# Four edits to a two-layer decoder trunk: padded arrays, joint splits of activations, one load on another queue, and two matmuls exchanged

## The chip, the cores and the metric

The kernel runs on one core of a Trainium2 chip. The metric is the device time of one execution in microseconds (us); before the change the median of three executions is 2053.09 us. The profile below is of one execution whose instructions span 2049.4 us. On the core, TensorE (PE) multiplies matrices and loads their stationary operands (PEld), VectorE (DVE) and ScalarE (ACT) do the elementwise work, GpSimd (POOL) does almost nothing, and SyncE (SP) issues the transfers.

## The reference, cut to what matters

```python
# D_MODEL 2048, SEQ 256, DEPTH 2, D_FF 8192, all float32
for layer in range(DEPTH):
    if layer < N_A:
        mix = short_conv_mixer(h, conv_w_in[layer], conv_w[layer], conv_w_out[layer])
    else:
        if layer == N_A:
            k_nope, k_pe, v = shared_latent_kv(h, kv_w_dkv, kv_norm_g, kv_w_ukv, cos, sin)
        mix = mla_mixer(h, ...)                       # 16 heads, causal softmax
    h = layer_norm(ALPHA * h + mix, ln_g[layer, 0], ln_b[layer, 0])
    h = layer_norm(ALPHA * h + sq_relu_mlp(h, mlp_w1[layer], mlp_w2[layer]), ...)

def sq_relu_mlp(x, w1, w2):
    return jnp.square(jax.nn.relu(x @ w1)) @ w2
```

The first layer mixes with a gated short convolution (projections of 2048 by 6144 and 2048 by 2048), the second with latent attention. Each has an MLP with 2048 by 8192 and 8192 by 2048 weights. Nearly all the work is in the products, and they run in float32.

## The kernel before, in words

**Products in two parts.** Every operand of a product is split into a rounded high part (type fp32r, made by a copy on ACT, line 111) and the low remainder (a subtraction on DVE, line 112; `split`). A product is then three terms, high by high, high by low and low by high. With the activations held as 512 columns, 256 high and 256 low, one K tile of 128 rows costs two matmuls: `high` (line 190, the weight's high part against all 512 columns) and `low` (line 194, the weight's low part against the first 256). `mm_run` runs 16 such pairs for one unit, 128 output rows; `whole` (lines 300 to 304) adds the two halves of the bank when it is done.

**Stages.** The input projection of the convolution has 48 units, the first three of them run side by side, on the input held in the arrays tagged a1 and a2 (8 K tiles each); its output projection has 16 units on z, in the array tagged b. An MLP goes over the 8192 hidden columns in 8 passes (`q` 0 to 7) of 8 units. The activations x are in the array tagged b, the hidden values of a pass in c. Pass 0 uses another form of product (`mm_wide`). The passes 1 to 7 call `products`, W1 for short below; after the W1 units of a pass come its W2 products, with the hidden values as stationary operand and 512 columns of weights moving (`dot`, lines 247 to 249). In the passes named in `FAST`, 1 to 6 of the first MLP and 1 to 7 of the second, half the W2 columns go through a product of the Strassen and Winograd kind, `down_fast`: seven products instead of eight for each pair of hidden tiles, over four pairs (`ps_f`, 84 matmuls). The other columns take the plain way (`down`, `ps_d`, 96 matmuls).

**Who prepares what.** `prepare` loads a weight (512 KB, line 132, on the SP queue) and splits it. For a pair of `down_fast` it loads two and forms combinations of them first: `raw_t`, two subtractions in `raw`, four splits, the last of which is written as `t` and is what the pair's first product reads. `hidden` (line 558) takes a unit out of its bank, applies relu and square, splits the result (`put_split`, lines 308 and 309) and, for every second unit of a FAST pass, forms four sums of the pair's quarters (lines 570 to 573, tile `sf`) and splits these, 512 columns, into `forms` (tag a2).

**Order.** The program is written stage by stage, but a planner orders each engine's instructions, and those of the SP queue, by simulated readiness. On the chip each engine and each queue takes its instructions strictly in the planned order.

**Where the arrays lie.** One pool holds, one after another, the residual (16,384 bytes for each partition), a1, a2, b, c, some arrays of 1,024 or 2,048 bytes, then the raw weights and the split weights (4,096 bytes each). A tag is as large as its largest user: 16,512 bytes for a1 and a2, 33,024 for b, 16,384 for c. So, modulo 512 bytes and counted from the residual, a1 begins at 0, a2 at 128, b at 256, c and the split weights at 0. Small constants stand ahead of the pool (`vec` 736 bytes, `col` 16), small statistics behind it, and behind these the tiles `sf` and `t4` of the FAST passes, where `t4` begins at 384.

**The end.** In the last pass, `to_out` first loads the gain and bias of the last norm, broadcast to all partitions, into the array tagged b (`gbt`, four transfers of 512 KB, line 869, on the POOL queue). It must wait for the last W1 matmul, which reads x from b. Then come `down_fast`, the rest of W2, and the norm.

Of the kernel before, what the change touches and what calls it, by code (L numbers as in the profile page):

```python
# [15 lines left out]
P = 128  # L16
# [24 lines left out]

C_G, C_B, C_CW, C_QG, C_KG, C_END = 0, 64, 128, 176, 180, 184
# [3 lines left out]
def trunk(ctx: ExitStack, tc: tile.TileContext, xT, vecs, w_in, w_out, w_kv, w_q, w_uk, w_uv,  # L46
# [10 lines left out]


# [171 lines left out]
    def products(n, x, group=0, cuts=()):  # L230
# [20 lines left out]
    def held(x, t):  # L251

        return [x[:, o + t * P:o + (t + 1) * P] for o in (0, T)]
# [33 lines left out]
    def down_fast(x, forms):  # L287
# [3 lines left out]
        for j in range(n):  # L291
            b, = take(1)
            a = {"11": held(x[2 * j], 0), "12": held(x[2 * j + 1], 0), "22": held(x[2 * j + 1], 1)}
            for i in range(4):
                a[f"S{i + 1}"] = [forms[:, j, o, i * P:(i + 1) * P] for o in range(2)]
# [16 lines left out]
    vec = const.tile([P, C_END], F32, name="vec")  # L312
# [5 lines left out]
    col = const.tile([P, 4], F32, name="col")  # L318
# [28 lines left out]
    class Norm:  # L347
# [35 lines left out]
        def widen(self, *tags):  # L383
# [4 lines left out]
            for i, tag in enumerate(tags):  # L388
                x = act.tile([P, n, 2 * W], F32R, tag=tag, name=f"xd{self.idx}_{i}")
# [85 lines left out]
    xhl = [t[:, k, :] for t in [act.tile([P, NC // 2, 2 * T], F32R, tag=a, name=f"xhl0_{a}") for a in ("a1", "a2")]  # L475
           for k in range(NC // 2)]

    first = act.tile([P, 2 * GROUP, 1024], F32, tag="b", name="first")
# [14 lines left out]
    zt = act.tile([P, NC, 2 * T], F32R, tag="b", name="z")  # L493
    z = [zt[:, k, :] for k in range(NC)]
    cbuf = act.tile([P, 2, 5, T + 2], F32, tag="c", name="cbuf")
# [27 lines left out]
    def mlp(idx, ln, begin, blocks, fast):  # L523
# [3 lines left out]
        xt = act.tile([P, NC, 2 * T], F32R, tag="b", name=f"xhl{idx}")  # L527
# [20 lines left out]
        for q in range(NQ):  # L548
            ht = act.tile([P, QC, 2 * T], F32R, tag="c", name=f"h{idx}_{q}")
            h = [ht[:, k, :] for k in range(QC)]  # L550
            forms = None
            if q in FAST[idx // 2]:
                forms = act.tile([P, QC // 2, 2, 4 * P], F32R, tag="a2", name=f"forms{idx}_{q}")
            if q == NQ - 1:
                begin(block)
            pair = []

            def hidden(m, ps, evac, *func):
                f = tmp.tile([P, T], F32, tag="fh", name="fh", bufs=3)
# [4 lines left out]
                put_split(h[m], f)  # L564
                pair.append(f)
                if forms is not None and m % 2:
                    (a11, a21), (a12, a22) = ((v[:, :P], v[:, P:]) for v in pair[-2:])
                    sf = fast.tile([P, 4, P], F32, tag="sf", name="sf")
                    s1, s2, s3, s4 = (sf[:, i, :] for i in range(4))
                    nc.vector.tensor_tensor(s1, a21, a22, ALU.add)  # L570
                    nc.vector.tensor_tensor(s3, a21, a11, ALU.subtract)
                    nc.vector.tensor_tensor(s2, s1, a11, ALU.subtract)
                    nc.vector.tensor_tensor(s4, a12, s2, ALU.subtract)
                    split(forms[:, m // 2, 0, :], forms[:, m // 2, 1, :], sf.rearrange("p i c -> p (i c)"))

            if q == 0:
# [15 lines left out]
                acc = act.tile([P, 2, D], F32, tag="a1", name=f"acc{idx}")  # L592
            else:
                for m, ps in enumerate(products(QC, xhl)):
# [56 lines left out]
    with tc.tile_pool(name="att", bufs=1) as ap:  # L651
        lat = act.tile([P, 2 * NK, 2 * T], F32R, tag="c", name="lat")
# [81 lines left out]
        ot = act.tile([P, H, 2 * T], F32R, tag="b", name="oT")  # L734
        oT = [ot[:, k, :] for k in range(H)]
        kq, vp = (act.tile([P, NC * W], F32, tag=a, name=f"kqv{a}") for a in ("a1", "a2"))
# [248 lines left out]
```

## Time and profile before

| | us |
|---|---|
| median of three executions | 2053.09 (2053.00 to 2053.85) |
| span of the profiled execution | 2049.4 |
| PE busy | 2030.6 |
| DVE busy | 1662.8 |
| ACT busy | 1194.1 |

The profiled execution's own time is known by its span alone. The median of the timed executions stands 3.7 us above that span; this is taken as what lies around the instructions, and any sum on the span has to have it added. A matmul's row in a timeline gives its start, its modelled duration and its kind. Matmuls overlap in the array, so the pace is read from start to start, and not from durations.

### The profile page before, as it was taken

Reading aid. Unit: us, or ns where it says so; the run is one execution under the profiler, and the core shown is the slowest. Engines: PE = TensorE matmul, PEld = TensorE weight load, DVE = VectorE, ACT = ScalarE, POOL = GpSimd, SP = SyncE. Lnnn points to the kernel's source line nnn. Section 1 sums busy time; section 2 is a strip of 40 time slices with the busy share of each in tenths; the row PEclk is TensorE's granted clock in tenths of the full one; section 3 lists DMA queues with packets and bytes.
Section 4 is the critical chain, followed back from the end, with each engine's and each line's share of the span. In section 5 each row is a group of like instructions: output and inputs, shape, how many; then the busy total and the mean of one; then the engine's idle time right before and its main releaser. Section 6 shows DMA issues by size and latency. Waiting matters only on the chain.

```text
span 2049.4 us, 30194 instructions
## 1 busy us (share of the span) xinstructions
PE 2030.6 (99%) x11208; PEld 1760.4 (86%) x11208; DVE 1662.8 (81%) x2602; ACT 1194.1 (58%) x1860; POOL 4.5 (0%) x25
## 2 busy tenths in 40 slices
PE   9999999999999999999999999999999999999997
PEld 8888888988888888888889998898888888888885
DVE  7667677678898988989788878776879888898988
ACT  6444445676566565655656665566656656566562
POOL 0000000000000000000000000000000000000000
PEclk9999999999999999999999999999999999999998
DMA  8666666564746557465755544656475664756653
GB/s 308 202 188 187 186 185 194 159 211 136 249 142 223 193 167 250 143 226 173 234 169 164 166 124 142 197 174 196 138 236 161 196 218 156 243 153 217 212 165 137
DMA packets 108003, 385.32 MB, mean 188 GB/s; under 512 B 11984, under 2 KB 13392, under 8 KB 107856
## 3 DMA queue, kind: packets, MB, share of 16 engines
q1 hardware_dynamic: 107136, 381.04, 58.7%
q0 software_dynamic: 576, 2.10, 0.3%
q8 instruction: 88, 1.44, 0.3%
q14 instruction: 59, 0.48, 0.1%
q10 hardware_dynamic: 144, 0.26, 0.0%
HBM read 381.25 MB, written 2.10 MB: 187 GB/s over the span
## 4 chain that ended last, share of the span: by engine, by line
PE 97%; DVE 1%; DMA 1%; issue 0%; ACT 0%; SPq 0%; DVEq 0%
PE ps_u L190 34%; PE ps_u L194 17%; PE ps_d L248 7%; PE ps_d L247 7%; PE ps_d L249 7%; PE ps_f L249 4%; PE ps_f L248 4%; PE ps_f L247 4%; PE ps_w L224 1%; PE ps_w L222 1%; PE ps_w L223 1%; PE ps_g L222 1%; PE ps_g L224 1%; PE ps_g L223 1%; PE ps_wo L190 1%; PE S L788 1%
## 5 line engine op out<-in xcount | busy, mean ns | idle before, releaser
L112 DVE TENSOR_TENSOR lo<-raw,hi 128x1024 fp32r<-128x1024 f32 x712 | 861.7, 1221 | 299.0 <-ACT hi L111 294.3
L111 ACT CAST hi<-raw 128x1024 fp32r<-128x1024 f32 x712 | 742.2, 1049 | 526.6 <-PE ps_u L190 289.5
L190 PE MATMUL ps_u<-xhl,hi 128*128 128x512 f32 x1792 | 632.2, 398 | 0.0
L194 PE MATMUL ps_u<-xhl,lo 128*128 128x256 f32 x1792 | 503.0, 281 | 0.0
L190 PEld LDWEIGHTS ps_u<-xhl,hi 128*128 128x128 f32 x1792 | 336.5, 188 | 82.3
L194 PEld LDWEIGHTS ps_u<-xhl,lo 128*128 128x128 f32 x1792 | 338.5, 189 | 0.5
L190 PE MATMUL ps_u<-xhl_a,hi 128*128 128x512 f32 x720 | 253.4, 396 | 0.0
L248 PE MATMUL ps_d<-lo,h 128*128 128x512 f32 x608 | 236.9, 390 | 0.0
L249 PE MATMUL ps_d<-hi,h 128*128 128x512 f32 x608 | 236.8, 390 | 0.0
L247 PE MATMUL ps_d<-hi,h 128*128 128x512 f32 x608 | 236.6, 389 | 0.0
L194 PE MATMUL ps_u<-xhl_a,lo 128*128 128x256 f32 x720 | 202.9, 282 | 0.0
L190 PEld LDWEIGHTS ps_u<-xhl_a,hi 128*128 128x128 f32 x720 | 135.2, 188 | 31.9
L194 PEld LDWEIGHTS ps_u<-xhl_a,lo 128*128 128x128 f32 x720 | 135.8, 189 | 0.0
L248 PEld LDWEIGHTS ps_d<-lo,h 128*128 128x128 f32 x608 | 114.1, 188 | 24.2 <-DVE lo L112 0.4
L247 PEld LDWEIGHTS ps_d<-hi,h 128*128 128x128 f32 x608 | 114.2, 188 | 24.0
L249 PEld LDWEIGHTS ps_d<-hi,h 128*128 128x128 f32 x608 | 114.1, 188 | 23.9
L111 ACT CAST hi_t<-raw_t 128x1024 fp32r<-128x1024 f32 x52 | 54.8, 1054 | 77.8 <-PE ps_u L190 41.8
L190 PE MATMUL ps_u<-z,hi 128*128 128x512 f32 x256 | 89.0, 392 | 0.0
L562 ACT ACTIVATE fh<-fh 128x256 f32<-128x256 f32 x112 | 46.4, 414 | 72.0 <-DVE fh L304 72.0
L222 PE MATMUL ps_w<-xd,hi 128*128 128x258 f32 x256 | 72.5, 284 | 0.0
L224 PE MATMUL ps_w<-xd,hi 128*128 128x258 f32 x256 | 72.5, 285 | 0.0
L223 PE MATMUL ps_w<-xd,lo 128*128 128x258 f32 x256 | 72.3, 282 | 0.0
(235 smaller groups left out, 3254.8 us busy)
## 6 DMA issues: line engine op xcount, KB each, us to landing
raw<-in_w_dram SPq DMA_DIRECT2D x408, 512.0 KB, 4.4
raw<-in_w2f_dram SPq DMA_DIRECT2D x104, 512.0 KB, 3.6
raw<-in_w_in_dram SPq DMA_DIRECT2D x90, 512.0 KB, 4.2
raw<-in_w_out_dram SPq DMA_DIRECT2D x32, 512.0 KB, 3.6
raw<-in_w_o_dram SPq DMA_DIRECT2D x32, 512.0 KB, 3.9
raw<-in_w_kv_dram SPq DMA_DIRECT2D x10, 512.0 KB, 4.3
raw<-in_w_q_dram SPq DMA_DIRECT2D x8, 512.0 KB, 4.5
raw<-in_w_uk_dram SPq DMA_DIRECT2D x8, 512.0 KB, 4.4
```

The source lines that it names most:

```text
L111: nc.scalar.copy(hi, src)
L112: nc.vector.tensor_tensor(lo, src, hi.bitcast(F32), ALU.subtract)
L190: nc.tensor.matmul(ps, w[blk // 8][0][:, blk % 8, :], x, start=first, stop=False)
L194: nc.tensor.matmul(ps[:, :T], w[blk // 8][1][:, blk % 8, :], x[:, :T], start=False, stop=last)
L222: nc.tensor.matmul(ps[:, :W], hi, x[k][:, :W], start=k == 0, stop=False)
L223: nc.tensor.matmul(ps[:, :W], lo, x[k][:, :W], start=False, stop=False)
L224: nc.tensor.matmul(ps[:, :W], hi, x[k][:, W:], start=False, stop=k == NC - 1)
L247: nc.tensor.matmul(ps, x[0], w[0], start=first, stop=False)
L248: nc.tensor.matmul(ps, x[0], w[1], start=False, stop=False)
L249: nc.tensor.matmul(ps, x[1], w[0], start=False, stop=last)
L562: nc.scalar.activation(f, f, AF.Relu)
L788: nc.tensor.matmul(S[:, at:at + n], qp[:, tok], kp[:, :n], start=False, stop=True)
```

## The change

**Arrays.** `array` gives each tag a fixed room that is a multiple of 512 bytes (16,896, 16,896, 33,280 and 16,384), and `vec`, `col` and `stats` are enlarged. The scratch for software transfers shrinks from 16,384 bytes to 2,048. All arrays of the main pool, the split weights and the FAST tiles then begin at the same offset modulo 512.

**Common splits.** In the passes 1 to 7 the two hidden tiles of a pair and the four sums are neighbours in one tile of 1,024 columns, and are split together: one copy on ACT and one subtraction on DVE instead of three each. High parts go to the array c and low parts to a2. In the one pass without sums (the first MLP's last) the pair's 512 columns are split together. The pair's tile has one buffer.

**One load on another queue.** The four `gbt` transfers go from the POOL queue to the SP queue.

**The exchange.** `products` passes `turn=2` for the first unit of the MLP passes 1 to 7: its third K tile has `low` ahead of `high`. That concerns 14 of the units.

```diff
+    ROOM = {"a1": 16896, "a2": 16896, "b": 33280, "c": 16384}
+    def array(tag, dtype, name, *dims):
+        n = int(np.prod(dims))
+        t = act.tile([P, ROOM[tag] // 4], dtype, tag=tag, name=name)[:, :n]
...
-    def mm_run(wps, x, k0, k1, nk, tiles_first=False):
+    def mm_run(wps, x, k0, k1, nk, tiles_first=False, turn=None):
...
         for k, (w, ps) in order:
+            if k == turn:
+                low(ps, w, k, x[k], False)
+                high(ps, w, k, x[k], False)
+                continue
             high(ps, w, k, x[k], k == 0)
             low(ps, w, k, x[k], k == nk - 1)
...
-            mm_run([(w, ps)], x, 0, NC, NC)
+            mm_run([(w, ps)], x, 0, NC, NC, turn=turn if i == 0 else None)
...
-    vec = const.tile([P, C_END], F32, name="vec")
+    vec = const.tile([P, 2 * P], F32, name="vec")[:, :C_END]
...
-    col = const.tile([P, 4], F32, name="col")
+    col = const.tile([P, COL], F32, name="col")
...
+            forms = [array(a, F32R, f"h{idx}_{q}_{a}", QC // 2, 8 * P) for a in ("c", "a2")] if q else None
...
-                put_split(h[m], f)
-                pair.append(f)
-                if forms is not None and m % 2:
-                    (a11, a21), (a12, a22) = ((v[:, :P], v[:, P:]) for v in pair[-2:])
-                    sf = fast.tile([P, 4, P], F32, tag="sf", name="sf")
...
-                    split(forms[:, m // 2, 0, :], forms[:, m // 2, 1, :], sf.rearrange("p i c -> p (i c)"))
+                if forms is None:
+                    put_split(h[m], f)
+                elif m % 2:
+                    hi, lo = (v[:, m // 2, :] for v in forms)
+                    src, cols = state["pair"], 4 * P
+                    if q in FAST[idx // 2]:
+                        cols = 8 * P
...
+                    split(hi[:, :cols], lo[:, :cols], src[:, :cols])
...
-                for m, ps in enumerate(products(QC, xhl)):
+                for m, ps in enumerate(products(QC, xhl, turn=2)):
...
-            nc.gpsimd.dma_start(gbt[:, n, :], gb[n].partition_broadcast(P))
-        stats = small.tile([P, 2, NB, 6], F32, tag="stats", name="stats", bufs=1)
+            nc.sync.dma_start(gbt[:, n, :], gb[n].partition_broadcast(P))
+        stats = small.tile([P, 2, NB, 10], F32, tag="stats", name="stats", bufs=1)[:, :, :, :6]
...
-    nc = _bacc.Bacc("TRN2", target_bir_lowering=False, num_devices=1)
+    nc = _bacc.Bacc("TRN2", target_bir_lowering=False, num_devices=1, dynamic_dma_scratch_size=2048)
```

More of the change, by code (lines that the diff above doesn't have):

```diff
@@ L228, in group_of, with products @@
         return [(take(), psum("ps_g")) for _ in range(n)]
-    def products(n, x, group=0, cuts=()):
+    def products(n, x, group=0, cuts=(), turn=None):
         ws = group_of(group)
@@ L294, in down_fast @@
             for i in range(4):
-                a[f"S{i + 1}"] = [forms[:, j, o, i * P:(i + 1) * P] for o in range(2)]
+                a[f"S{i + 1}"] = [v[:, j, (4 + i) * P:(5 + i) * P] for v in forms]
             for p, l, r in FACTORS:
@@ L523, in mlp @@
     def mlp(idx, ln, begin, blocks, fast):
-        xt = act.tile([P, NC, 2 * T], F32R, tag="b", name=f"xhl{idx}")
+        xt = array("b", F32R, f"xhl{idx}", NC, 2 * T)
         xhl = [xt[:, k, :] for k in range(NC)]
```

54 lines of the change are left out of this document (31 added, 23 removed).

## The prediction

> **What bounds the kernel now.** I read the page first: the shares of the engines and the chain that ended last.
>
> ```profile
> span 2049.4 us, 30194 instructions
> PE 2030.6 (99%) x11208; PEld 1760.4 (86%) x11208; DVE 1662.8 (81%) x2602; ACT 1194.1 (58%) x1860; POOL 4.5 (0%) x25
> ...
> PE 97%; DVE 1%; DMA 1%; issue 0%; ACT 0%; SPq 0%; DVEq 0%
> ```
>
> The chain is matmuls for 97% of the span, so an edit pays where it alters the pace of the matmuls or one of the few places where they wait. Hence the second view, PE's timeline, read from start to start. It is shown where a W2 stretch ends and a pass of W1 begins.
>
> ```profile
> 458.46 0.39 PE L249 MATMUL ps_d<-hi,h 128*128 128x512 f32 x1
> 458.69 0.39 PE L190 MATMUL ps_u<-xhl,hi 128*128 128x512 f32 x1
> ...
> 459.03 0.40 PE L190 MATMUL ps_u<-xhl,hi 128*128 128x512 f32 x1
> ...
> 459.38 0.40 PE L190 MATMUL ps_u<-xhl,hi 128*128 128x512 f32 x1
> ...
> 459.74 0.40 PE L190 MATMUL ps_u<-xhl,hi 128*128 128x512 f32 x1
> ...
> 460.09 0.40 PE L190 MATMUL ps_u<-xhl,hi 128*128 128x512 f32 x1
> ```
>
> Only the high matmul of each K tile is shown; a low one lies between. From the second K tile (459.03) on, three K tiles take 0.35, 0.36 and 0.35 us, 1.06 together and 0.353 each. The same instructions run faster elsewhere. Here are the first matmul of a K tile and the same place 16 K tiles, one unit, later, in a usual pass and in the first MLP's last:
>
> ```profile
> 740.83 0.40 PE L190 MATMUL ps_u<-xhl,hi 128*128 128x512 f32 x1
> ...
> 746.48 0.40 PE L190 MATMUL ps_u<-xhl,hi 128*128 128x512 f32 x1
> ...
> 1000.40 0.39 PE L190 MATMUL ps_u<-xhl,hi 128*128 128x512 f32 x1
> ...
> 1005.95 0.39 PE L190 MATMUL ps_u<-xhl,hi 128*128 128x512 f32 x1
> ```
>
> That is 5.65 us a unit against 5.55, with nothing waiting in either. So the pace of high and low in turn has a slow pattern and an even one, and which one runs depends on how a stretch was entered. The 12 passes that follow W2 without a gap (1 to 6 of both MLPs) are in the slow one; the last pass of each MLP starts after other work and is in the even one.
>
> **The exchange of two matmuls** neither adds nor removes work. It can only change the pattern. If it takes, each of the 12 passes gains 8 units x 0.10 = 0.8 us, 9.6 us in all. The nearest rows are two places where two low matmuls already stand together (a row with x2):
>
> ```profile
> 13.75 0.40 PE L194 MATMUL ps_g<-xhl_a,lo 128*128 128x256 f32 x2
> ...
> 15.04 0.40 PE L190 MATMUL ps_g<-xhl_a,hi 128*128 128x512 f32 x1
> ...
> 16.10 0.40 PE L190 MATMUL ps_g<-xhl_a,hi 128*128 128x512 f32 x1
> ...
> 284.38 0.40 PE L194 MATMUL ps_u<-z,lo 128*128 128x256 f32 x2
> ...
> 284.61 0.40 PE L190 MATMUL ps_u<-z,hi 128*128 128x512 f32 x1
> ...
> 284.96 0.39 PE L190 MATMUL ps_u<-z,hi 128*128 128x512 f32 x1
> ```
>
> After the first, three K tiles again take 1.06 us (15.04 to 16.10): nothing won. After the second a K tile takes 0.35 (284.61 to 284.96) and the duration drops to the even pattern's 0.39. One for and one against; in the change two high matmuls follow the two low ones, which neither row has. I take the gain in full, since the even pattern is the one that holds wherever a stretch on the arrays b was entered with a break, and keep nothing as the other end. The two passes that are even already may fall into the slow pattern: 0 to +1.6 us, taken as 0.
>
> **Padding.** `ps_f` is where operands with different offsets meet: `forms` lies 128 bytes off the weights modulo 512, `t4` 384, while in `ps_d` both operands are at 0.
>
> ```profile
> 763.44 0.39 PE L247 MATMUL ps_f<-t,h 128*128 128x512 f32 x1
> ...
> 782.93 0.40 PE L247 MATMUL ps_d<-hi,h 128*128 128x512 f32 x1
> ...
> 1499.64 0.39 PE L249 MATMUL ps_d<-hi,h 128*128 128x512 f32 x1
> ...
> 1505.99 0.39 PE L247 MATMUL ps_d<-hi,h 128*128 128x512 f32 x1
> ```
>
> The 84 matmuls of `ps_f` take 19.49 us, 0.232 each. The 28 of `ps_d` from 1499.64 to 1505.99 take 0.2268 each, with the same 512 moving columns. If equal offsets bring `ps_f` to that pace it takes 19.05, and some 0.05 for finding it: 0.39 less in each of 12 passes, 4.7 us (the thirteenth is below). The lower bound is nothing.
>
> The convolution's input has its second half in a2, also 128 off.
>
> ```profile
> 75.44 0.40 PE L190 MATMUL ps_u<-xhl_a,hi 128*128 128x512 f32 x1
> ...
> 81.07 0.40 PE L190 MATMUL ps_u<-xhl_a,hi 128*128 128x512 f32 x1
> ```
>
> A unit takes 5.63 there. With equal offsets it should have one of the two patterns: the slow 5.65 (45 units x 0.02 = +1.0 us) or the even 5.55 (-3.6). I take the slow one, which its aligned first half already shows, and keep both ends.
>
> A rule of the Trainium skill speaks against this part: "SBUF — State Buffer", section "Who interferes with whom", gives PE two independent read ports and says that PE never waits on anyone, by which offsets are worth nothing. The two paces of 0.232 and 0.2268 for equal shapes do not look like that, though no row here separates the offset from the order of products. By that rule the sum below would be 3.7 us higher.
>
> **Joint splits.** What they remove and add, by group:
>
> ```profile
> L309 DVE TENSOR_TENSOR h<-fh,h 128x256 fp32r<-128x256 f32 x128 | 53.4, 419 | 2.3 <-ACT h L308 1.7
> L112 DVE TENSOR_TENSOR forms<-sf,forms 128x512 fp32r<-128x512 f32 x52 | 35.5, 683 | 0.0
> L112 DVE TENSOR_TENSOR lo<-raw,hi 128x1024 fp32r<-128x1024 f32 x712 | 861.7, 1221 | 299.0 <-ACT hi L111 294.3
> ...
> L111 ACT CAST hi<-raw 128x1024 fp32r<-128x1024 f32 x712 | 742.2, 1049 | 526.6 <-PE ps_u L190 289.5
> ```
>
> The weight's split of 1,024 columns gives the price of the joint one. A pair costs DVE 2 x 0.42 + 0.68 = 1.52 us now and 1.22 after; ACT copies in 1.05. Both lie beside PE, so the sum is nothing as long as the cover holds. It is thin at one place, the fourth pair of `ps_f`, whose weights DVE finishes last:
>
> ```profile
> 861.54 0.68 DVE L112 TENSOR_TENSOR forms<-sf,forms 128x512 fp32r<-128x512 f32 x1
> ...
> 863.28 0.68 DVE L112 TENSOR_TENSOR t<-raw,t 128x512 fp32r<-128x512 f32 x1
> ...
> 864.58 0.39 PE L247 MATMUL ps_f<-t,h 128*128 128x512 f32 x1
> ```
>
> `t` is written at 863.28 + 0.68 = 863.96 and PE reads it at 864.58: 0.62 us of slack. After, PE comes 63 x 0.0052 = 0.33 earlier, and in this stretch DVE has a split that is 1.22 - 0.68 = 0.54 longer, less one of 0.42 and its gap that falls away: some 0.15 more. That leaves 0.1: no wait, but no reserve either. The single buffer of the pair's tile makes the next unit's add wait for the split; behind it on DVE and ACT stand weight splits, and PE would notice only when banks run out, a unit (5.6 us) later. Nothing for that. Bounds of the whole part: 0, and what the second rival says.
>
> **`gbt` on SP.**
>
> ```profile
> 1990.99 2.23 POOL L869 DMA_DIRECT2D gbt<-in_gb_dram  x4 [1038.46 <-PE ps_u L194]
> ...
> 1993.17 8.60 DMA raw<-in_w2f_dram
> ...
> 2006.15 0.50 PE L247 MATMUL ps_f<-t,h 128*128 128x512 f32 x1 [0.78 <-ACT t L111]
> 2008.08 0.55 PE L248 MATMUL ps_f<-t,h 128*128 128x512 f32 x1 [1.44 <-DVE t L112]
> 2008.42 0.63 PE L249 MATMUL ps_f<-t,h 128*128 128x512 f32 x1
> 2008.85 0.63 PE L247 MATMUL ps_f<-hi,h 128*128 128x512 f32 x1
> ```
>
> The last weights of the fourth pair share the engines with 2 MB of `gbt` and land after 8.60 us. PE could begin the pair 63 x 0.232 = 14.6 us after W1's end, at about 2005.1, and does its second matmul at 2008.08 instead of 2005.35: 2.7 us. For about eight matmuls it then runs at 0.43 instead of 0.23: 1.6 us. The stall costs 4.3. On SP the four transfers can be issued only once the last W1 matmul is done, as on POOL. If the load follows them in one queue it lands a little earlier than when it shares with them, I estimate by 1 us out of the 8.60; the bounds are +2 and -4.3 (the whole stall). What is queued behind the four on SP are the fourth pair's second load and then all remaining W2 loads. The Trainium skill, "DMA: Bandwidth & Descriptors", section "Issuing engines are not separate DMA queues", holds that the issuing engine only changes the issue time; by it this term is 0 and the sum 1 us higher.
>
> **The sum.** -9.6 - 4.7 + 1.0 + 0 - 1.0 = -14.3 us on the profiled span of 2049.4: 2035.1, and with the 3.7 around it 2038.8.
>
> **Rivals.** *The exchange does nothing*: W1 stays in, or falls back into, the slow pattern. For it speaks the row at 13.75. 2038.8 + 9.6 = 2048.4.
>
> *The fourth pair waits* (this one is slower). If DVE gets to the joint split only after `t`, then ACT's copy (1.05) and the split (1.22) come after 863.96, which ends them at 866.23, where PE now needs them at 864.25: 1.98 us in each of 12 passes, 23.8 us, 2062.6. It decides from 14.3 / 12 = 1.2 us a pass. Against it: the row at 861.54, where the sums' split begins 1.7 us ahead of `t`. For it: 0.1 us of reserve.
>
> *SP is held up.* If the four transfers are planned ahead of the second pair's loads, which SP now issues from 1968.53 on,
>
> ```profile
> 1968.53 2.60 SPq L132 DMA_DIRECT2D raw<-in_w2f_dram  x2
> ```
>
> these go out after 1993 and land, behind 2 MB, at about 2002. From landing to the first product takes 6.3 us (2001.77 to 2008.08), so PE gets the second pair at 2008.3, where it wants it 21 matmuls after W1's end, at about 1995.6: 12.7. A pair costs DVE five pieces of 1.22 and three of 0.68, which overlap a little, some 7 us, and PE 4.9, so the two further pairs add about 2 each. Less the old 4.3 this is +12.4, and 2038.8 + 1.0 + 12.4 = 2052.2. Against it: the planner orders by readiness, and the loads are ready 20 us sooner.
>
> *Offsets do not matter* (the SBUF rule): `ps_f` and the convolution keep their paces: 2038.8 + 4.7 - 1.0 = 2042.5.
>
> **Chances.** All as forecast 0.50, the exchange does nothing 0.18, the fourth pair waits 0.12, SP held up 0.09, offsets do not matter 0.08, the rest 0.03. The likeliest has 2034 (an even convolution) to 2043 of its own. The range for 8 in 10 reaches over all cases but the wait: below by the even convolution and the whole stall gone, with some left out, 2032; above to SP held up and its spread, 2054. A change of 0.2%, 4.1 us, is about what a measurement can tell here, so faster means below 2049: the forecast, the offsets case and some 0.12 of the idle exchange, 0.70. Within 0.2% fall SP held up and the rest of the idle exchange, 0.15. Slower, 0.15.
>
> **What would show it.** The exchange: W1 units at 5.55 in passes 1 to 6. Padding: `ps_f` at 19.1 from first to last matmul. Joint splits: PE without an idle row at the fourth pair. `gbt`: the row of the last w2f load below 8.60 and an earlier end of the stall. Wrong would be the prediction if W1 units stay at 5.65, or if a wait of over 1.2 us a pass stands ahead of a `ps_f` matmul.

## The result and the profile after

The changed kernel takes 2035.26 us (median of four executions, 2034.58 to 2039.59) against 2053.32 for the kernel before beside it: 0.9913 of it, with a 95% interval of 0.9899 to 0.9927. The forecast was 2038.8 in a range of 2032 to 2054. The profiled execution spans 2032.7 us, 16.7 less than the one of before; the sum had said 14.3.

In every execution that followed, of the kernel before too, the time stands 1.7 to 2.2 us above the span. The profiled execution of the kernel before has no time of its own on record; with 2.0 us its time would be about 2051.4 (an estimate). So the 3.7 us that the prediction added seem to come from setting a median beside the span of another, faster execution. Below, spans are compared with spans. Executions of one kernel differ: the spans of the kernel before go from 2049.4 to 2055.7 us, those of the changed kernel from 2032.5 to 2037.5, so a difference of a few us between two single profiles is read stage by stage, not from the span.

The page of the changed kernel, its span, the engines' shares and the chain that ended last:

```profile
span 2032.7 us, 30055 instructions
...
PE 2013.6 (99%) x11208; PEld 1756.4 (86%) x11208; DVE 1653.9 (81%) x2494; ACT 1179.3 (58%) x1752; POOL 2.3 (0%) x21
...
PE 96%; DVE 2%; DMA 1%; issue 1%; ACT 0%; DVEq 0%; SPq 0%; ACTq 0%
```

PE is the bound as before, by the same number of matmuls. They are issued faster. PE's timeline in the first MLP's fourth pass (start, modelled duration, line, operands), from the first matmul of W1 over the exchange to the first of `ps_f`, of `ps_d` and of the next pass:

```profile
713.28 0.39 PE L200 MATMUL ps_u<-xhl,hi 128*128 128x512 f32 x1
...
713.85 0.40 PE L204 MATMUL ps_u<-xhl,lo 128*128 128x256 f32 x2
714.09 0.63 PE L200 MATMUL ps_u<-xhl,hi 128*128 128x512 f32 x2
...
718.85 0.39 PE L200 MATMUL ps_u<-xhl,hi 128*128 128x512 f32 x1
...
724.39 0.39 PE L200 MATMUL ps_u<-xhl,hi 128*128 128x512 f32 x1
...
757.67 0.39 PE L261 MATMUL ps_f<-t,h_c 128*128 128x512 f32 x1
...
776.75 0.39 PE L261 MATMUL ps_d<-hi,h_c 128*128 128x512 f32 x1
...
798.51 0.39 PE L200 MATMUL ps_u<-xhl,hi 128*128 128x512 f32 x1
```

The two rows with x2 are the exchange: two low matmuls, then two high ones. From the second unit on a unit takes 5.54 to 5.55 us (718.85 to 724.39), W1 of the pass 44.4 instead of 45.2, and `ps_f` 19.08 (757.67 to 776.75) instead of 19.49. That repeats in all 12 passes.

Not every stretch gained. The same view at the starts of two neighbouring units (one K tile in where a stretch starts late) of the convolution, z, the first MLP's last pass and oT:

```profile
75.63 0.39 PE L200 MATMUL ps_u<-xhl_a,hi 128*128 128x512 f32 x1
...
81.18 0.39 PE L200 MATMUL ps_u<-xhl_a,hi 128*128 128x512 f32 x1
...
287.17 0.40 PE L200 MATMUL ps_u<-z,hi 128*128 128x512 f32 x1
...
292.82 0.40 PE L200 MATMUL ps_u<-z,hi 128*128 128x512 f32 x1
...
975.05 0.40 PE L200 MATMUL ps_u<-xhl,hi 128*128 128x512 f32 x1
...
980.70 0.40 PE L200 MATMUL ps_u<-xhl,hi 128*128 128x512 f32 x1
...
1252.64 0.40 PE L200 MATMUL ps_u<-oT,hi 128*128 128x512 f32 x1
...
1258.30 0.40 PE L200 MATMUL ps_u<-oT,hi 128*128 128x512 f32 x1
```

The convolution is in the even pattern (5.55). The other three are in the slow one (5.65 and 5.66), and they were even before. Stage by stage, from the starts of the stages in both timelines:

| stretch | change of its length, us | forecast |
|---|---|---|
| start, until 26 us | +0.8 | 0 |
| convolution's units | -3.5 | +1.0, bounds -3.6 and +1.0 |
| z | +1.5 | 0 |
| W1 in 12 passes | -9.8 | -9.6 |
| W2 in 12 passes (`ps_f` -4.95, `ps_d` -0.57) | -5.5 | -4.7 |
| W1 in the first MLP's last pass | +0.8 | 0, bound +0.8 |
| oT | +1.4 | 0 |
| last pass behind W1 (`ps_f` -3.5, `ps_d` and norm +0.7) | -2.7 | -1.0, bounds +2 and -4.3 |
| the rest | +0.3 | 0 |
| sum | -16.7 | -14.3 |

### The profile page after: what moved, and what is told of

Its sections match the earlier page's. It is cut to its first block, busy times and chain, and to the rows that moved or that the text cites. A ratio compares the mean times of both kernels' runs of the same rounds, so it can differ in the third digit from the quotient of the medians.

```text
span 2032.7 us, 30055 instructions
## 1 busy us (share of the span) xinstructions
PE 2013.6 (99%) x11208; PEld 1756.4 (86%) x11208; DVE 1653.9 (81%) x2494; ACT 1179.3 (58%) x1752; POOL 2.3 (0%) x21
## 3 DMA queue, kind: packets, MB, share of 16 engines
q8 instruction: 88, 1.44, 0.3%
## 4 chain that ended last, share of the span: by engine, by line
PE 96%; DVE 2%; DMA 1%; issue 1%; ACT 0%; DVEq 0%; SPq 0%; ACTq 0%
PE ps_u L200 33%; PE ps_u L204 17%; PE ps_d L262 7%; PE ps_d L261 7%; PE ps_d L263 7%; PE ps_f L262 4%; PE ps_f L263 4%; PE ps_f L261 4%; PE ps_w L238 1%; PE ps_w L236 1%; PE ps_w L237 1%; PE ps_g L238 1%; PE ps_g L236 1%; PE ps_g L237 1%; DMA raw<-in_w2f_dram 1%
## 5 line engine op out<-in xcount | busy, mean ns | idle before, releaser
L261 PE MATMUL ps_d<-hi,h_c 128*128 128x512 f32 x480 | 186.8, 389 | 0.0
L262 PE MATMUL ps_d<-lo,h_c 128*128 128x512 f32 x480 | 186.7, 389 | 0.0
L263 PE MATMUL ps_d<-hi,h_a 128*128 128x512 f32 x480 | 186.6, 389 | 0.0
L262 PEld LDWEIGHTS ps_d<-lo,h_c 128*128 128x128 f32 x480 | 90.1, 188 | 18.9 <-DVE lo L122 0.3
L263 PEld LDWEIGHTS ps_d<-hi,h_a 128*128 128x128 f32 x480 | 90.1, 188 | 18.7
L261 PEld LDWEIGHTS ps_d<-hi,h_c 128*128 128x128 f32 x480 | 90.1, 188 | 18.7
L582 ACT ACTIVATE sf<-sf 128x256 f32<-128x256 f32 x112 | 46.7, 417 | 86.9 <-DVE sf L319 86.6
L262 PE MATMUL ps_f<-lo,h_c 128*128 128x512 f32 x208 | 81.2, 390 | 0.2 <-DVE lo L122 0.2
L263 PE MATMUL ps_f<-hi,h_a 128*128 128x512 f32 x208 | 81.1, 390 | 0.0
L261 PE MATMUL ps_f<-hi,h_c 128*128 128x512 f32 x208 | 80.8, 389 | 0.0
```

What stands on the lines that cost most here:

```text
L261: nc.tensor.matmul(ps, x[0], w[0], start=first, stop=False)
L262: nc.tensor.matmul(ps, x[0], w[1], start=False, stop=False)
L263: nc.tensor.matmul(ps, x[1], w[0], start=False, stop=last)
L582: nc.scalar.activation(f, f, AF.Relu)
```

## The experiments

Theory A was the prediction's: the order of two matmuls flips PE between two patterns, equal offsets set the pace of products whose operands lay apart, the joint splits cost and gain nothing, and `gbt` matters a little at the end. The parts were run by themselves or taken out of the changed kernel, then their mechanisms were varied.

**The exchange alone, on the arrays of before.**

```diff
-                for m, ps in enumerate(products(QC, xhl)):
+                for m, ps in enumerate(products(QC, xhl, turn=2)):
```

> The kernel before with the exchange alone; offsets, splits and gbt stay. Theory A, the exchange flips PE between its two patterns wherever the operands lie: W1 units of passes 1 to 6 fall from 5.65 to 5.55 (12 x -0.84 = -10.1 us), and the two last passes, even already, flip to the slow one (up to 2 x +0.8): span 2040 to 2041, some 2043.8 to 2045. Rival B, the even pattern needs equal offsets too: W1 units stay at 5.65, nothing gained, 2053.

0.9968 of before (0.9958 to 0.9978), 2046.78 us, span 2046.0. PE's timeline, W1 of the fourth pass and two neighbouring units of the first MLP's last pass:

```profile
717.63 0.39 PE L190 MATMUL ps_u<-xhl,hi 128*128 128x512 f32 x1
...
762.02 0.39 PE L251 MATMUL ps_f<-t,h 128*128 128x512 f32 x1
...
981.04 0.40 PE L190 MATMUL ps_u<-xhl,hi 128*128 128x512 f32 x1
...
986.69 0.40 PE L190 MATMUL ps_u<-xhl,hi 128*128 128x512 f32 x1
```

W1 takes 44.4 in all 12 passes (-9.8 together) and both last passes became slow (+0.8 each), as theory A had it; equal offsets are not needed. The span is still 5 us above the theory's 2040 to 2041. Three things outside the theory took part of the gain back: z ran in the slow pattern this time (+1.6), `ps_f` takes 19.59 instead of 19.50 behind the even W1 (W2 together +1.0), and the last pass behind W1 was 2.1 us longer. In that pass PE waits 1.82 us for a weight in `ps_d`, at 2020.82, and its granted clock is 0.51 in the window from 2022 to 2024.

**The padding alone.**

```diff
-                x = act.tile([P, n, 2 * W], F32R, tag=tag, name=f"xd{self.idx}_{i}")
+                x = array(tag, F32R, f"xd{self.idx}_{i}", n, 2 * W)
...
-    vec = const.tile([P, C_END], F32, name="vec")
+    vec = const.tile([P, 2 * P], F32, name="vec")[:, :C_END]
```

> The kernel before with the padding alone (equal offsets; no exchange, separate splits, gbt on POOL). Theory A, offsets set PE's pace: ps_f 19.5 -> 19.1 in 13 passes (-5.2), convolution units 5.63 -> 5.55 or 5.65 (-3.6 or +1.0), W1 stays at 5.65: span 2040 to 2046. Rival C, offsets cost nothing and ps_f's gain in the changed kernel comes from the way PE enters it: ps_f stays at 19.5 because W1 ahead of it is slow, span 2049. Time outside the span: 2.1 us instead of 3.7 if it hangs on the smaller scratch area, 3.7 if it hangs on gbt's queue.

0.9978 (0.9969 to 0.9988), 2048.10 us, span 2048.1. The same timeline, first matmul of `ps_f` and of `ps_d` in the fourth pass:

```profile
763.12 0.40 PE L257 MATMUL ps_f<-t,h 128*128 128x512 f32 x1
...
782.22 0.39 PE L257 MATMUL ps_d<-hi,h 128*128 128x512 f32 x1
```

`ps_f` takes 19.10 with W1 still at 45.2 ahead of it: its gain (12 x 0.39 = 4.7 us) comes from the offsets and not from the way PE enters it. Rival C falls. The span is above the theory's 2040 to 2046 all the same: the convolution's first 24 units ran at 5.65 and the 20 after 161 us at 5.55, z and oT ran in the slow pattern (+2.9 together), and the last `ps_f` took 25.5 instead of 23.9. Beside the profiled execution of the kernel before that leaves 1.3 us in the spans; the medians of this round, 2054.25 and 2048.10, lie 6.2 apart.

**The changed kernel without the exchange.**

```diff
-                for m, ps in enumerate(products(QC, xhl, turn=2)):
+                for m, ps in enumerate(products(QC, xhl)):
```

> The changed kernel without the exchange. Theory A: W1 units of passes 1 to 6 go back to 5.65 (+10.1 us), the last pass of the first MLP back to 5.55 (-0.8), the last of the second between 0 and +0.8; ps_f stays at 19.1: span 2042 to 2043, time 2044 to 2045. Rival C, ps_f's pace comes from the even W1 ahead of it: ps_f also goes back to 19.5, 5 us more, 2049 to 2050.

0.9961 (0.9946 to 0.9975), 2044.67 us, span 2042.5. W1 is back at 45.2, the last pass of the first MLP back at 44.6, `ps_f` stays at 19.1, so rival C falls here too. The exchange is worth 9.4 us in the medians here and 9.8 in the spans.

**`gbt` on SP alone, and `gbt` back on POOL in the changed kernel.** The two were run apart.

```diff
-            nc.gpsimd.dma_start(gbt[:, n, :], gb[n].partition_broadcast(P))
+            nc.sync.dma_start(gbt[:, n, :], gb[n].partition_broadcast(P))
```

> The kernel before with gbt on SP alone. Theory Q, the queue makes the gain at the end: last ps_f 23.9 -> 20.4, span 2046, time 2048 to 2050. Theory D, the gain at the end comes from DVE, which no longer has a split of the sums among the last pair's pieces, and from a stall short enough that PE keeps its clock: the load lands some 0.3 us earlier, the stall of about 2 us and the half clock stay, last ps_f 23.3 to 23.9, span 2049, time 2052 to 2053. Time outside the span 2.1 us if it hangs on POOL's transfers, else 3.7.

0.9991 (0.9982 to 1.0000), 2051.29 us; the last `ps_f` takes 22.1 instead of 23.9, between the two theories. Of the chain that ended last the load of the last pair's second weights, then VectorE's and PE's timelines:

```profile
1994.70 9.09 DMA raw<-in_w2f_dram
```

```profile
2000.23 0.69 DVE L112 TENSOR_TENSOR forms<-sf,forms 128x512 fp32r<-128x512 f32 x1 [0.69 <-ACT forms L111]
2003.81 1.23 DVE L154 TENSOR_TENSOR raw_t<-raw,raw 128x1024 f32<-128x1024 f32 x1 [2.89 <-DMA raw<-in_w2f_dram]
...
2007.63 0.50 PE L247 MATMUL ps_f<-t,h 128*128 128x512 f32 x1 [1.52 <-ACT t L111]
2008.81 0.50 PE L248 MATMUL ps_f<-lo,h 128*128 128x512 f32 x1 [0.44 <-DVE lo L112]
```

The load lands at 2003.79, 12.5 us after W1's end at 1991.3; in the kernel before it was 11.3 (2001.77 after 1990.5). So it lands later, and yet the stretch is shorter. What differs is the planned order, on two engines. On VectorE the split of the last sums now runs at 2000.23, while VectorE waits for the load; in the kernel before it stood among the pieces made from the load:

```profile
2005.61 0.68 DVE L112 TENSOR_TENSOR forms<-sf,forms 128x512 fp32r<-128x512 f32 x1
```

On PE the second matmul that must wait reads `lo`, which VectorE finishes at 2008.76; in the kernel before it reads `t`, the last of the pieces (the row at 2008.08). And PE keeps its clock: it is 1.00 from 2008 to 2012, where the kernel before has 0.60 and 0.55 in the same two windows.

The other direction:

```diff
-            nc.sync.dma_start(gbt[:, n, :], gb[n].partition_broadcast(P))
+            nc.gpsimd.dma_start(gbt[:, n, :], gb[n].partition_broadcast(P))
```

> The changed kernel with gbt's four transfers on POOL again. Theory Q, SP's queue makes the gain at the end: last ps_f 22 to 23.9 instead of 20.4, time 2037 to 2039. Theory D, the gain comes from DVE's order in the last pair and from PE keeping its clock: the load lands 0.3 us later, last ps_f 20.4 to 21, time 2035 to 2036.

0.9934 (0.9917 to 0.9950), 2040.12 us, span 2037.0; the last `ps_f` takes 25.9. VectorE's timeline, PE's, and the windows (length, PE busy, PEld, DVE, ACT, POOL, granted clock, DMA share, GB/s):

```profile
1987.96 1.23 DVE L164 TENSOR_TENSOR raw_t<-raw,raw 128x1024 f32<-128x1024 f32 x1 [4.37 <-DMA raw<-in_w2f_dram]
...
1991.77 1.22 DVE L122 TENSOR_TENSOR h_a<-sf,h_c 128x1024 fp32r<-128x1024 f32 x1
```

```profile
1992.74 0.49 PE L261 MATMUL ps_f<-t,h_c 128*128 128x512 f32 x1 [2.20 <-ACT t L121]
1994.78 0.80 PE L262 MATMUL ps_f<-t,h_c 128*128 128x512 f32 x1 [1.55 <-DVE t L122]
```

```profile
1994.00:1996.00 2.00, 1.22 (x3) 1.03 (x4) 2.00 (x4) 0.99 (x2) 0.00 (x0) 0.50 0.84 207
1996.00:1998.00 2.00, 2.00 (x7) 1.52 (x6) 2.00 (x2) 0.63 (x1) 0.00 (x0) 0.50 0.88 346
```

And the same place in the changed kernel, VectorE, PE and a window:

```profile
1985.64 1.23 DVE L122 TENSOR_TENSOR h_a<-sf,h_c 128x1024 fp32r<-128x1024 f32 x1 [1.17 <-ACT h_c L121]
1987.53 1.23 DVE L164 TENSOR_TENSOR raw_t<-raw,raw 128x1024 f32<-128x1024 f32 x1 [0.67 <-DMA raw<-in_w2f_dram]
```

```profile
1991.37 0.50 PE L261 MATMUL ps_f<-t,h_c 128*128 128x512 f32 x1 [0.35 <-ACT t L121]
1992.54 0.50 PE L262 MATMUL ps_f<-lo,h_c 128*128 128x512 f32 x1 [0.20 <-DVE lo L122]
```

```profile
1994.00:1996.00 2.00, 2.00 (x11) 1.64 (x10) 1.96 (x4) 1.05 (x1) 0.00 (x0) 1.00 0.69 256
```

On POOL the load lands 11.9 us after W1's end, on SP 11.0: 0.9 us. The rest is read as order and clock. With `gbt` on POOL, VectorE idles 4.37 us for the load and has the joint split `h_a`, which needs no load, behind it, among the pieces. With `gbt` on SP the split fills the wait. PE's order differs as in the other pair of kernels: the second wait is for `t` on POOL and for `lo`, which is ready sooner, on SP. PE then idles 0.35 and 0.20 instead of 2.20 and 1.55, which is 3.2 us, and its granted clock stays at 1.00 instead of 0.50: eleven matmuls from 1995.38 on start 0.43 us apart instead of 0.23, some 2.2 us. Neither theory of these two experiments had it whole: the queue makes the gain, 5.5 us in `ps_f`, of which 0.9 is the transfer itself. No run changed an order and left the queue as it was, so the orders' share is read from the timelines and not shown by an experiment of its own. That the planner moves the split because SP's queue delays the load in its own reckoning is argued; that the orders differ is shown. The Trainium skill, "DMA: Bandwidth & Descriptors", section "Issuing engines are not separate DMA queues", has it that transfers share the same engines whoever issues them. For the landing the traces do not go far from that (0.9 us earlier in one pair of kernels, 1.3 later in the other).

Whether the clock falls does not follow from the length of the waits. In the kernel with the exchange alone PE waits a little longer at the same place than in the kernel before (there 0.78 and 1.44, clock 0.60 and 0.55 afterwards), and keeps a clock of 1.00 through 2008:

```profile
2000.78 0.49 PE L251 MATMUL ps_f<-t,h 128*128 128x512 f32 x1 [1.01 <-ACT t L111]
2002.71 0.50 PE L252 MATMUL ps_f<-t,h 128*128 128x512 f32 x1 [1.44 <-DVE t L112]
```

So the clock's part of a stall is not a price to count on.

**Where the exchange stands.**

```diff
-            if k == turn:
+            if k in (turn or ()):
...
+TURNS = {1: {1: (3,), 2: (4,), 3: (2, 8), 4: (2, 9), 5: (2, 10), 6: (), 7: ()},
+         3: {1: (1,), 2: (5,), 3: (8,), 4: (2, 3), 5: (2, 4), 6: (12,), 7: ()}}
```

> The changed kernel with the exchange at other K tiles of the first W1 unit, pass by pass. First MLP: pass 1 at the K tile 3, pass 2 at 4, pass 3 at 2 and 8, pass 4 at 2 and 9, pass 5 at 2 and 10, passes 6 and 7 none. Second MLP: pass 1 at 1, 2 at 5, 3 at 8, 4 at 2 and 3, 5 at 2 and 4, 6 at 12, 7 none. All W1 passes start in the slow pattern but pass 7 of the first MLP. Theory T, each exchange flips the pattern, wherever it stands: one exchange gives 44.4 us a pass, two or none 45.2. Rival P, it works only at one place of the slow pattern's three K tiles: 2, 5 and 8 give 44.4, the tiles 1, 3, 4 and 12 45.2. Rival R, an exchange always ends in the even pattern: two give 44.4 as well. By T the span is that of the changed kernel plus 6 to 7 passes x 0.84 less 0.84: 2037 to 2038.

2041.97 us (median of two executions), span 2041.5, above theory T's 2037 to 2038. W1 of a pass, from its first matmul to the next stage's first:

| exchanged K tiles | W1 of the pass, us |
|---|---|
| 2 (changed kernel) | 44.4 |
| 5; 8 | 44.4; 44.4 |
| none | 45.2 |
| 1; 3; 4; 12 | 45.2; 45.2; 45.2; 45.2 |
| 2 and 8; 2 and 9; 2 and 10 | 45.2; 45.2; 45.2 |
| 2 and 4 | 45.2 |
| 2 and 3 | 44.4 |

PE's timeline, the start of a unit and of the next, first in the pass with the K tile 3 exchanged, then in the one with 5:

```profile
471.73 0.40 PE L202 MATMUL ps_u<-xhl,hi 128*128 128x512 f32 x1
...
477.38 0.40 PE L202 MATMUL ps_u<-xhl,hi 128*128 128x512 f32 x1
...
1521.16 0.39 PE L202 MATMUL ps_u<-xhl,hi 128*128 128x512 f32 x1
...
1526.71 0.39 PE L202 MATMUL ps_u<-xhl,hi 128*128 128x512 f32 x1
```

Theory T holds for a second exchange at 4, 8, 9 or 10: it leads out of the even pattern back to the slow one. One at 3, right behind the first, does not. For the first exchange rival P holds: out of the slow pattern, which repeats every three K tiles, only one at 2, 5 or 8 leads to the even one, and those at 1, 3, 4 and 12 do nothing. Rival R falls. So the change's third K tile is one of three kinds of place, and at the places tried of the two other kinds the exchange is worth nothing.

**The loaded operand moved by 128 bytes.**

```diff
-            forms = [array(a, F32R, f"h{idx}_{q}_{a}", QC // 2, 8 * P) for a in ("c", "a2")] if q else None
+            forms = [array(a, F32R, f"h{idx}_{q}_{a}", QC // 2, 8 * P, at=32) for a in ("c", "a2")] if q else None
```

> The changed kernel with both halves of the activations and sums that W2's products load as weights moved on by 128 bytes; the W2 weights that stream stay where they are. Theory A, PE's pace is set by the offset between the loaded and the streamed operand: the matmuls of ps_f go from 0.227 to 0.232 us (19.1 -> 19.5 in 13 passes) and so do 1,440 of ps_d (each pass's 96: 21.76 -> 22.3), together 5 + 7.5 us, time 2047 to 2048. Rival M, what costs is a change of offset from one matmul to the next, of which this kernel has none within ps_f or ps_d: nothing, 2035.

0.9973 (0.9962 to 0.9984), 2047.61 us. First matmul of `ps_f`, of `ps_d` and of the next pass:

```profile
762.60 0.39 PE L261 MATMUL ps_f<-t,h_c 128*128 128x512 f32 x1
...
782.12 0.39 PE L261 MATMUL ps_d<-hi,h_c 128*128 128x512 f32 x1
...
804.41 0.39 PE L200 MATMUL ps_u<-xhl,hi 128*128 128x512 f32 x1
```

`ps_f` takes 19.52 (0.232 a matmul) and `ps_d` 22.29 instead of 21.76 (0.232 instead of 0.227). All matmuls of the two have the same 128 bytes between loaded and streamed operand here, so a change of it from one matmul to the next is not what costs: rival M falls, and theory A gave the size. No run moved both operands by the same 128 bytes, so that the distance counts, and not each array's own offset, is argued and not shown. The Trainium skill, "SBUF — State Buffer", section "Who interferes with whom", gives PE two independent read ports and lets it wait on nobody. This measurement differs, by 12 us in W2's products of a kernel in which only addresses have moved, and it decides.

**Separate splits again.**

```diff
-                elif m % 2:
+                else:
                     hi, lo = (v[:, m // 2, :] for v in forms)
-                    src, cols = state["pair"], 4 * P
+                    src, o = state["pair"], m % 2 * T
+                    split(hi[:, o:o + T], lo[:, o:o + T], src[:, o:o + T])
...
-                    split(hi[:, :cols], lo[:, :cols], src[:, :cols])
+                        split(hi[:, 4 * P:], lo[:, 4 * P:], src[:, 4 * P:])
```

> The changed kernel with three splits a pair again (two of 256 columns, one of the 512 columns of sums) in place of one of 1,024. Prediction's reading: nothing on PE; DVE busy about 14 us more, PE ahead of the fourth pair with 0.1 to 0.3 us of slack, time 2035. Rival, the joint split is what shortened the end: the last pair's pieces have the sums' split of 0.68 among them again, the stall grows by some 0.7 to 1 us and PE falls back to half its clock behind it, last ps_f 21.5 to 23.5 instead of 20.4, time 2036 to 2038.

0.9907 (0.9891 to 0.9924), 2035.33 us against 2035.26. VectorE is busy 3.7 us more (1657.6) and ScalarE 18.3 (1197.6), and PE notices next to nothing (0.3 us in one pass). The last `ps_f` stays at 20.3, since its splits run before the load is there: the rival falls. VectorE's rows overlap, which is part of why its busy time moved by less than the 14 us expected. `t` is written 0.03 to 0.33 us ahead of the fourth pair's first matmul in 11 of the 12 passes, and 0.35 after it in the twelfth. With the joint split it is 0.11 to 0.12 in 11 passes and 0.01 in one. The first MLP's fifth pass in the changed kernel:

```profile
856.43 0.68 DVE L122 TENSOR_TENSOR t<-raw,t 128x512 fp32r<-128x512 f32 x1
...
857.23 0.39 PE L261 MATMUL ps_f<-t,h_c 128*128 128x512 f32 x1
```

That first matmul reads the high part of `t`, which ScalarE writes. The low part, which VectorE writes, is read by the next one, 0.23 us later (in the kernel before the wait at 2006.15 is for ScalarE's `t` and the one at 2008.08 for VectorE's). So the reserve of VectorE is some 0.35 us, and not 0.12.

**The exchange where the changed kernel is slow.**

```diff
-    summed(ln, products(NC, z), residual)
+    summed(ln, products(NC, z, turn=2), residual)
...
-                for m, ps in enumerate(products(QC, xhl, turn=2)):
+                for m, ps in enumerate(products(QC, xhl, turn=None if (idx, q) == (1, NQ - 1) else 2)):
...
-        yield from products(NC - WO_G, oT)
+        yield from products(NC - WO_G, oT, turn=2)
```

> The changed kernel with the exchange also in the first unit of z's and of oT's products, which run in the slow pattern there, and without it in the last pass of the first MLP, which it made slow. Theory T: z 84.5 -> 82.9, oT 73.5 -> 72.1, the pass 45.4 -> 44.6, together -3.8 us: span 2029, time 2031. Rival, the pattern of z and oT is drawn anew in every execution, so that a fixed exchange helps as often as it hurts: between 2031 and 2035, differing from execution to execution.

0.9906 (0.9891 to 0.9920), 2033.21 us. The last pass is back at 44.6. z and oT are as slow as before the edit. oT had come into its first unit in the even pattern this time, and the exchange made it slow. That is the rival's outcome for oT. In z the exchange left the even first unit even, and so it did in the second MLP's last pass of the changed kernel (44.5), which it made slow on the arrays of before (45.3). So out of the even pattern, too, an exchange at the same K tile does not always lead to the other one. In z the slow pattern comes later: at the seam to the second unit two matmuls take 0.36 and 0.34 us from start to start instead of 0.23, and it begins behind this break, with the exchange or without. That the pattern changes between executions of one kernel is inferred: there is one profile of each. Over the profiled executions with equal offsets and no exchange in the stretch, the convolution's first 24 units are even in 4 of 10, z in 1 of 9, oT in 1 of 9; with the offsets of before z was even in 2 of 3 and oT in 3 of 3. In these stretches a break stands at or near the entry, and the place in the pattern at which the exchange falls is not the same each time. In the 12 passes that follow W2 without a gap it is.

**Other orders.** The units' products in groups of high and low parts.

```diff
+PLANS = {1: {1: ((16,), (1,)), 2: ((16,),), 3: ((2,),), 4: (("snake",),), 5: ((4,),), 6: (2, (1,)), 7: ((1,),)},
+         3: {1: ((16,), 2, (1,)), 2: ((16,), 1, (1,)), 3: ((16,), 3, (1,)), 4: ((8, 8), (1,)), 5: ((4, 4), (1,)),
+             6: ((2, 2), (1,)), 7: (("snake",),)}}
```

> The changed kernel with other orders of the products of W1's units, pass by pass. First MLP: pass 1, the first unit with all 16 high parts and then all 16 low ones, the others alternating; pass 2, all units so; pass 3, all units in twos (two high, two low); pass 4, all units with every other K tile exchanged; pass 5, all units in fours; pass 6 as in the change; pass 7 alternating. Second MLP: first unit all high then all low, and the second alternating with the K tile 2 (pass 1), 1 (pass 2) or 3 (pass 3) exchanged; the first 8, 4 or 2 K tiles of the first unit grouped high then low (passes 4, 5, 6); pass 7, every other K tile exchanged. Theory T, the pattern is set by the time at which PE enters the alternation: some of the grouped entries give even units (44.4 a pass) and others slow ones (45.2), and the separated order itself runs at 0.2267 + 0.120, that is 5.55 a unit and a little for each turn between the two kinds, 44.4 to 45. Rival, alternation is slow whenever it does not start with an exchange: all grouped entries give 45.2.

2041.68 us, a single execution, span 2039.9.

| order | W1 of the pass, us |
|---|---|
| every unit all high, then all low | 44.5 |
| twos; fours | 44.6; 44.9 |
| every other K tile exchanged (two passes) | 44.6; 44.7 |
| first unit separated, rest alternating | 45.1 |
| first unit separated, second with 1 exchanged | 44.4 |
| the same with 2; with 3 | 45.1; 45.1 |
| first 8, 4 or 2 K tiles grouped, rest alternating | 45.2; 45.2; 45.2 |

Neither has it whole. All grouped entries that go on in plain alternation are slow, as the rival said; theory T expected some of them even. But an exchange does not suffice either: behind a separated unit only the one at 1 leads to the even pattern, and those at 2 and 3 do not. Neighbouring units of that pass:

```profile
1516.86 0.39 PE L237 MATMUL ps_u<-xhl,hi 128*128 128x512 f32 x1
...
1522.41 0.39 PE L237 MATMUL ps_u<-xhl,hi 128*128 128x512 f32 x1
```

Straight behind W2 it was 2, 5 or 8. So the place of a working exchange depends on what PE did before. A separated unit is then a way to make that known: in this pass its matmuls run at the steady paces of their kinds, 0.227 and 0.120 us, soon after their start.

**Half of `gbt` early.**

```diff
+        early = fast.tile([P, NB // 2, 2 * BW], F32, tag="gb0", name="early")
+        for n in range(NB // 2):
+            nc.sync.dma_start(early[:, n, :], gb[n].partition_broadcast(P))
```

> The changed kernel with the first two of gbt's four transfers issued at the start of the second MLP into a tile of their own; only the last two remain behind W1's end. Theory L, what is left of the stall at the last ps_f is the weights' transfer beside gbt's: the load lands 1 to 2 us earlier, last ps_f 20.4 -> 19.1 to 19.5, time 2034 to 2034.3. Rival, the stall comes from DVE's pieces: 20.4 stays, 2035.3.

0.9902 (0.9888 to 0.9917), 2034.15 us; the 1.1 us against the changed kernel lie within the intervals, so the profile decides. The last `ps_f` takes 19.1 and has no stall: theory L. PE's timeline shows what comes late next, a weight of the remaining W2 stretch, 0.95 us, and `ps_d` with the norm gives 0.2 of the gain back:

```profile
2007.91 0.50 PE L262 MATMUL ps_d<-lo,h_c 128*128 128x512 f32 x1 [0.95 <-DVE lo L122]
```

**All of it together: a settled entry.** e10, no exchange in the two last passes, and in the convolution, z and oT a second unit separated and a third with its K tile 1 exchanged.

```diff
+SETTLE = ((1,), (16,), 1, (1,))
...
-    summed(ln, products(NC, z), residual)
+    summed(ln, products(NC, z, plans=SETTLE), residual)
...
-                for m, ps in enumerate(products(QC, xhl, turn=2)):
+                for m, ps in enumerate(products(QC, xhl, turn=2 if q < NQ - 1 else None)):
...
-        yield from products(NC - WO_G, oT)
+        yield from products(NC - WO_G, oT, plans=SETTLE)
```

> The changed kernel with gbt half early (as in e10), without the exchange in each MLP's last pass, and with a settled entry in the convolution's, z's and oT's products: their second unit all high parts and then all low ones, their third alternating with the K tile 1 exchanged, which in e9 led to the even pattern. Theory T: the convolution's units from 30 us on at 5.55 (nothing against the changed kernel's profile, where chance had it so already; -2.5 us where it is slow), z 84.5 -> 82.9, oT 73.5 -> 72.3, first MLP's last pass -0.8, end -1.4: span 2027 to 2028, time 2029 to 2030.5. Rival, the entry ahead of those units is not the same in every execution and the exchange hits the wrong place: z and oT stay at 84.5 and 73.5, time 2032 to 2034.

0.9876 (0.9859 to 0.9892), 2029.10 us, 6 less than the changed kernel, and its four executions lie within 0.85 us (2028.56 to 2029.41) where the changed kernel's spread over 5.0. Neighbouring units of z and of oT on PE's timeline:

```profile
292.51 0.39 PE L235 MATMUL ps_u<-z,hi 128*128 128x512 f32 x1
...
298.06 0.39 PE L235 MATMUL ps_u<-z,hi 128*128 128x512 f32 x1
...
1266.64 0.39 PE L235 MATMUL ps_u<-oT,hi 128*128 128x512 f32 x1
...
1272.19 0.39 PE L235 MATMUL ps_u<-oT,hi 128*128 128x512 f32 x1
```

Both are even (5.55), and the convolution is too: theory T, and the rival falls for the profiled execution; the narrow spread of the four times speaks for the others. The span is 2027.3: z -1.5, the first MLP's last pass -0.8, oT -1.3, the last `ps_f` -1.3. It is the fastest kernel of this study.

## Why the prediction was right, and where not

**The exchange** was right in its mechanism and its size: -9.8 in 12 passes against -9.6. The doubt, whether two high matmuls behind two low ones keep the even pattern, was settled by the rows of the fourth pass and by the run without the exchange. The bound "the two passes that are even already may fall into the slow pattern" came true for one of them (+0.8), taken as 0. What the prediction did not see is that the place matters: at the K tiles 1, 3, 4 and 12 the rival "the exchange does nothing" would have been the outcome. No row of the prediction speaks for the third K tile over another, so that the change exchanged this one is luck as far as the prediction goes.

**Padding.** `ps_f` and the first matmuls of `ps_d` gave 5.5 us against 4.7 (`ps_f` alone 5.0), and the moved operand showed that the offset is the cause. For the convolution I took "the slow one, which its aligned first half already shows"; the profiled execution had the even one, at the other bound. That choice cannot be called a mistake or a hit: by the other executions it falls either way. The step that was missing is z and oT. I took the even pattern there as given, since it was there before; it was not part of the change, and the kernels with equal offsets nearly always have it slow (+2.9). Why they do is open.

**Joint splits** were worth nothing on PE, as said, and `t` is written 0.12 us ahead of the fourth pair's first matmul where the prediction left 0.1. Two steps to that 0.1 were off. The terms 0.54, 0.42 and a gap give at most 0.12 more for VectorE, not 0.15; and what VectorE writes is read by the second matmul, 0.23 later, so the reserve was about three times what was thought. The rival with the wait of 1.98 us did not come: VectorE reaches the joint split ahead of `t` in every pass.

**`gbt`** is the term that was mis-sized: -1.0 taken, -2.7 measured in the last pass, inside the bounds. Of the 2.7, some 0.4 is the faster pace of `ps_f`, which the sum left out for this pass. By the run with `gbt` back on POOL the queue itself is worth 4.8 us there (5.5 in `ps_f`, less 0.8 behind it), more than the stall of 4.3 that bounded it; on the arrays of before it is worth 1.2. The reasoning, "it lands a little earlier than when it shares with them", gave the wrong cause. The landing is worth 0.9; the rest goes with the order of VectorE's and PE's work, and with the stall and the clock after it. The 1.6 of the stall that the prediction put down to slow matmuls is not one to count on: after waits no shorter the kernel with the exchange alone has none. The rival of SP held up did not come: the four transfers are issued at W1's end, from 1976.73 on, and the second pair's loads from 1955.90 on. (Its 6.3 us from landing to the first product run to the pair's second matmul; the first is at 2006.15, 4.4 after the landing.)

**The 3.7 us** around the span should have been about 2.0, as the executions of these runs show. It cancels against nothing: with 2.0 the same sum would have been 2037.1, nearer to the 2035.26 measured. Within the sum errors did cancel: the convolution came out 4.5 us lower than taken, the last pass 1.7 and W2 0.8, z and oT 2.9 higher and the first MLP's last pass 0.8.

## What to carry to other kernels

Read a saturated TensorE from start to start, and compare equal instructions at different places: about 2% of the pace of W1 and of `ps_f` lay in the order of two matmuls and in addresses, with no wait in any row. Where a pattern depends on how a stretch is entered, look at it in several executions before counting on it, and settle the entry rather than the place of an exchange. When a transfer moves to another queue, look at what the engine behind it has planned between the landing and the use; that order can be worth more than the landing.

## What was not expected of the hardware

Loaded and streamed operands 128 bytes apart modulo 512 cost 5.4 ns for each matmul of 512 columns (0.2322 against 0.2268), while 256 apart cost nothing: with the arrays of before x lies 256 from the weights, and W1 has the same two paces there, 5.65 and 5.55, as with equal offsets. The slow pattern of alternating matmuls repeats every three K tiles, and among the places tried an exchange leads out of it at one of the three only. Why, no run here shows. After two waits of 2.20 and 1.55 us PE's granted clock was 0.50 in the three windows of 2 us from 1994 to 2000, and after 0.78 and 1.44 it was 0.60 and 0.55 in two; after 1.01 and 1.44, after 1.52 and 0.44, and after 0.35 and 0.20 it stayed at 1.00. So the sum of the waits alone does not decide.
